# A plain product for the first two groups of a Strassen-tiled step, with its start, its norm steps and its last plans put in another order

## The chip, the cores and the metric

One core of a Trainium2 chip. TensorE (PE; its weight loads are listed as PEld) multiplies, VectorE (DVE) and ScalarE (ACT) do the elementwise work, GpSimd (POOL) and SyncE (SP) mainly issue transfers. Each engine works through its own queue of instructions in order and waits at semaphores for what other engines or transfers have to finish. The metric is device microseconds of one execution. The kernel before took 2694.85 us (median of three runs, 2691.01 to 2695.05).

## The reference

One layer for a prompt of 2048 tokens and, beside it, a sample of 64 tokens with a state; D is 1024, and everything is float32:

```
h = rms_norm(x, g_pre);  vA, bA, cA, zA, q, f, iv, zB, gA, gB = split(h @ w_in)     # ten parts of 1024
u = cA * vA;  yA = (silu(zA) * bA * causal_conv3(u)) @ w_a_out
fg = lb + (1 - lb) * sigmoid(f)
o = hgrn2_scan(state, silu(q) * scale, 1 - fg, iv, log(fg))     # 8 heads, chunks of 64 tokens
yB = (rms_norm_per_head(o) * g_onorm * silu(zB)) @ w_b_out
out = (sigmoid(gA) * yA + sigmoid(gB) * yB) @ w_o
x = x + rms_norm(out, g_post)
y = x + (p @ w_ple_proj) * sigmoid(rms_norm(x, g_ple) @ w_ple_gate)
```

Outputs are y, the last two columns of u and the states after the scan, for prompt and sample.

## The kernel before

**Tiles.** The 2112 tokens are put side by side and cut into three blocks of 704 (`BN`), each block into two halves of 352 (`HN`). Activations lie with features on partitions: tile k holds features 128k to 128k+127 of the 704 tokens. Every float32 operand is split into a hi part (a cast to fp32r, ACT) and a lo part (the difference, DVE; `split`, L184), and a product is three matmuls of 352 columns, hi x hi, hi x lo and lo x hi. Nearly all activations live in one ring of 52 slots (`rt`). PSUM has five banks for the large products (`psg`, named pg) and three (`psa`, named pa) for the scan, the norms and ple.

**Groups.** The ten projections are made by `sgroup` in Strassen-Winograd form: two output columns i1 and i2 of 128 features, times two halves of the tokens, need seven products (`PRODUCTS`) of 4 k-steps x 3 matmuls = 84 matmuls, where the plain form needs 96. The products use sums of weight blocks (S1 to S4) and of activations (T1 to T4). `combined` loads the weights; in block 0 it makes the four weight sums (L295), splits them and keeps sums and lo parts in DRAM (`keep_sum`, `lows`); blocks 1 and 2 load the kept ones (`kept_w`). The activation operands, a list by k for each of B11, T3, T1, T2, B21, T4 and B22, come from `operands`: for each of four pairs (tiles i and i+4) two scaled x tiles (L636), four differences of half tiles (L643 and following) and the splits.

**Stages of a block.** `path_b` goes through the 8 heads: `head_prep` makes three groups (forget gate and query FF/QQ, then the value and output gate), the scan steps of the head hang as `hooks` behind products, and after the first group of a head one step of `fills` is made, which is one group of `gates` (sigmoid of GA and GB, eight groups in all, results spilled to DRAM). `path_a` makes vA, cA, zA, bA and the convolution. Then come w_a_out, w_b_out and w_o (`merge` in block 0, `merge_in_turn` later), `final_norm` (two rms norms with a column sum on TensorE, L581, a power on POOL, and a spread over the partitions by TensorE, L565) and `final_gate`, the last product. `ple` is the small product p @ w_ple_proj: eight steps of 2 halves x 2 k x 3 = 12 matmuls (L951 to L953), each half evicted from its pa bank (L958), the tile spilled to DRAM unless the block is the last.

**Start.** SP's queue loads p of block 0, four ple weights, twelve tiles of x by token (`rows`), four ple weights, then x by feature in pairs with p of block 1 behind the second tile, then weights. Row sums of squares (ACT squares, DVE sums) give the first norm, whose reciprocal root is made on POOL (L555) and spread (L565, `spread_all`). Four steps of block 0's ple are issued between the row sums, the other four behind the spread and the first pair of operands. Then all of p of block 1 is split, and then the pairs 2 to 4 of operands. The first group (GA 0 and 1) runs `by_k`: for each k two steps of block 1's ple and then k of four products.

**Order.** A scheduler places the instructions on the engines by data and priority (`tc.high_priority`); `placed()` holds an instruction behind the last matmul that was issued, `behind_all(marks)` behind the marked instructions. `hook()` pops one entry of `hooks` after each product; `spread_out` fills that list with counts of steps of a generator, here those of `final_norm`, to be run one entry per hook. In blocks 0 and 1 the norm runs amid the gates of the next block; in the last block its first steps (final_norm of half 0) run in the last w_o products (from `(W_O, 4)`) and go on in the last ple, that of half 1 follows amid the last products of `final_gate`. There, too, ACT squares `sum_squares` (L599, L600) and evicts ple (L958), both in its one queue, and DVE adds x (L1088).

Of the kernel before, what the change touches and what calls it, by code (L numbers as in the profile page):

```python
# [82 lines left out]
def hybrid_step(  # L83
# [150 lines left out]
    behind = []  # L234
    last, hooks, copies = [None], [], [None]
# [25 lines left out]
    def steps(gen, n):  # L261
        return lambda: run(gen, n)

# [21 lines left out]
    def combined(i1, i2, first, ahead):  # L285

        with tc.high_priority() if ahead else nullcontext():
# [59 lines left out]
    def sgroup(i1, i2, hc, sink, first, mid=None, by_k=False, ahead=True, between=None):  # L347

        with behind_all(behind.pop(0) if behind else ()):
            w = combined(i1, i2, first, ahead)
# [14 lines left out]
        if by_k:  # L367
            for k in range(KH):
                if between is not None:
                    between()  # L370
                for n in range(4):
                    product(n, (k,))
        for n, (bank, _, _, _, stop) in enumerate(PRODUCTS):
# [9 lines left out]
            if n == 3:  # L383
                u2 = got[0]
                V.tensor_tensor(u2, u2, ps["b"], ALU.add)
            elif n == 4:
                sink(0, 0, ps["a"], None)
            elif n == 5:
                sink(1, 0, u2, ps["c"])
                V.tensor_tensor(got[1], got[1], got[2], ALU.add)  # L390
                sink(1, 1, u2, got[1])
            elif n == 6:
                sink(0, 1, u2, ps["d"])
# [18 lines left out]


# [5 lines left out]
    def operand_of(raw, name, k):  # L419

        (b11, b12), (b21, b22) = ([half(raw[i], h) for h in range(2)] for i in (k, k + KH))
        if name == "B21":
            V.tensor_tensor(b11, b12, b11, ALU.subtract)
        if name == "T2":
# [127 lines left out]
    def rstd_of(ms_ap, out_ap, scale, start=0):  # L552
        V.tensor_scalar(out_ap, ms_ap, scale, EPS, ALU.mult, ALU.add)
        shape = [out_ap.shape[0], out_ap.shape[1]]
        G.tensor_tensor(out_ap, out_ap, mhalf[start : start + shape[0], :].to_broadcast(shape), ALU.pow)  # L555

# [71 lines left out]
    def operands(hc, rs, load, marks=None):  # L628


        for i in range(KH):
            pair = []
            with behind_all(marks[i - 2][1:] if marks and i >= 2 else ()):
                for k in (i, i + KH):
                    xk = load(k)
                    V.scalar_tensor_tensor(xk, xk, g_pre[:, k : k + 1], rs, ALU.mult, ALU.mult)  # L636
                    pair.append(xk)
            (b11, b12), (b21, b22) = ([half(x, h) for h in range(2)] for x in pair)
            one = rt(dt=F32R)
            split(b11, half(one, 0), half(one, 1))  # L640
            hc["B11"].append((half(one, 0), half(one, 1)))
            s = rt()
            V.tensor_tensor(half(s, 1), b22, b12, ALU.subtract)  # L643
            V.tensor_tensor(half(s, 0), b12, b11, ALU.subtract)
            hi, lo = split_rt(s)
            hc["T3"].append((half(hi, 1), half(lo, 1)))
            hc["T1"].append((half(hi, 0), half(lo, 0)))
            t = rt()
            V.tensor_tensor(half(t, 0), b22, half(s, 0), ALU.subtract)
            V.tensor_tensor(half(t, 1), b21, half(t, 0), ALU.subtract)  # L650
            hi, lo = split_rt(t)
            hc["T2"].append((half(hi, 0), half(lo, 0)))
            hc["T4"].append((half(hi, 1), half(lo, 1)))
            hi, lo = rt(dt=F32R), rt(dt=F32R)
            done = split(pair[1], hi, lo)
            if marks is not None:
                marks.append(done)
            hc["B21"].append((half(hi, 0), half(lo, 0)))
            hc["B22"].append((half(hi, 1), half(lo, 1)))
            yield  # L660
# [5 lines left out]
    def gates(bl, hc, kept, first, between=None):  # L666

        for kind in (GA, GB):
            for j in range(0, KB, 2):
                outs = [rt(), rt()]  # L670

                def sink(c, h, x, y):
                    if c == 0:
# [644 lines left out]
```

## Time and profile before

| what | value |
|---|---|
| median of the runs | 2694.85 us |
| the profiled execution: time | 2695.89 us |
| the profiled execution: span | 2694.2 us |
| busy share PE, DVE, ACT, POOL | 98%, 64%, 54%, 13% |
| DMA, mean | 274 GB/s |
| mean granted clock of TensorE | 0.990 |
| PE's busy tenths, first and last of 40 slices | 6 and 9 |

The span goes from the first instruction to the last of the one execution that the profiler recorded; its time is a little more than its span. A row of the timeline or of a group reads: start, duration, engine, line, operation, output<-input, shape; in square brackets the idle time of the engine before it and what ended that. A row of windows reads: the stretch, its length, then busy time and count of each engine (or of PE alone), the granted clock (1 is full speed) and the DMA share and GB/s. Matmuls overlap, so that the duration of one is about twice the distance between two starts; the distances are used here.

### The profile page before, as it was taken

The page shows a single profiled execution, that of the slowest core. Times are in us where ns is not written, and L with a number is a line of the kernel's source. Part 1 is how long each engine was busy: PE and PEld are TensorE (multiplying, and loading weights), DVE is VectorE, ACT ScalarE, POOL GpSimd, SP SyncE. Part 2 cuts the span into 40 slices and gives each one's busy share as a digit, 9 for nine tenths or more (in the row PEclk, how much of TensorE's full clock was granted, in tenths as well). Part 3 has the DMA queues.
Part 4 walks back from the last instruction along what each step waited for, and adds up shares of the span by engine and source line. Part 5 has one row for each costly group of instructions (what it writes and reads, how often), then busy time and mean ns, then how long its engine had stood idle before and what let it go on. Part 6 is the DMA issues. An engine that isn't in the chain of part 4 may idle for free. (4 is left out here: it accounts for less than half of the span.)

```text
span 2694.2 us, 47741 instructions
## 1 busy us (share of the span) xinstructions
PE 2635.0 (98%) x16724; PEld 2607.4 (97%) x16724; DVE 1726.9 (64%) x3340; ACT 1459.7 (54%) x2792; POOL 351.1 (13%) x649
## 2 busy tenths in 40 slices
PE   6999999999999999999999999999999999999989
PEld 5999999999999999999999999999999999999989
DVE  6788888899776543566645577554355564447756
ACT  4665565454334554566645555454466654446654
POOL 1000000110341211011112210021010000001011
PEclk8999999999999999999999999999999999999999
DMA  6767777898997898767789998599876668889855
GB/s 236 267 243 264 267 239 272 281 335 289 338 385 265 314 329 276 243 221 223 223 271 356 388 330 290 182 353 311 269 227 216 222 223 263 274 280 331 281 187 196
DMA packets 362674, 738.16 MB, mean 274 GB/s; under 512 B 44128, under 2 KB 46720, under 8 KB 362432
## 3 DMA queue, kind: packets, MB, share of 16 engines
q1 hardware_dynamic: 325440, 591.34, 65.5%
q0 software_dynamic: 36704, 143.70, 14.7%
q8 instruction: 132, 2.16, 0.3%
q14 instruction: 110, 0.90, 0.1%
q10 hardware_dynamic: 288, 0.05, 0.0%
HBM read 530.43 MB, written 204.49 MB: 273 GB/s over the span
## 5 line engine op out<-in xcount | busy, mean ns | idle before, releaser
L363 PE MATMUL pg<-r,hi 128*128 128x352 f32 x3360 | 1113.6, 332 | 11.9 <-DVE r L411 2.9
L364 PE MATMUL pg<-r,hi 128*128 128x352 f32 x3360 | 1089.8, 324 | 3.9 <-DVE r L184 3.9
L365 PE MATMUL pg<-r,lo 128*128 128x352 f32 x2400 | 778.1, 325 | 3.7 <-DMA lo<-low 3.0
L214 ACT CAST hi<-raw 128x512 fp32r<-128x512 f32 x724 | 447.1, 621 | 579.0 <-PE pg L364 204.3
L363 PEld LDWEIGHTS pg<-r,hi 128*128 128x128 f32 x3360 | 633.8, 189 | 21.5 <-issue 5.1
L364 PEld LDWEIGHTS pg<-r,hi 128*128 128x128 f32 x3360 | 634.5, 189 | 6.7 <-DVE r L184 6.7
L365 PEld LDWEIGHTS pg<-r,lo 128*128 128x128 f32 x2400 | 453.4, 189 | 5.6 <-DMA lo<-low 3.8
L365 PE MATMUL pg<-r,s 128*128 128x352 f32 x960 | 310.4, 323 | 2.7 <-DMA s<-low 2.7
L492 PE MATMUL pg<-r,hi 128*128 128x352 f32 x896 | 290.4, 324 | 0.3 <-DVE r L184 0.3
L491 PE MATMUL pg<-r,hi 128*128 128x352 f32 x896 | 290.2, 324 | 0.4 <-ACT hi L184 0.3
L493 PE MATMUL pg<-r,lo 128*128 128x352 f32 x756 | 245.1, 324 | 2.4 <-DVE lo L184 2.4
L184 ACT CAST hi<-raw 128x512 fp32r<-128x512 f32 (+1 forms) x232 | 141.7, 614 | 173.9 <-PE pg L364 40.7
L184 DVE TENSOR_TENSOR r<-r,r 128x352 fp32r<-128x352 f32 (+3 forms) x270 | 167.5, 640 | 73.1 <-ACT r L184 72.4
L184 DVE TENSOR_TENSOR lo<-raw,hi 128x512 fp32r<-128x512 f32 (+1 forms) x232 | 156.9, 680 | 87.0 <-ACT hi L184 70.7
L184 ACT CAST r<-r 128x352 fp32r<-128x352 f32 (+3 forms) x270 | 148.5, 581 | 72.2 <-DVE r L650 17.0
L365 PEld LDWEIGHTS pg<-r,s 128*128 128x128 f32 x960 | 180.7, 188 | 3.3 <-DMA s<-low 3.3
L459 PE MATMUL pg<-r,hi 128*128 128x352 f32 x560 | 182.1, 327 | 0.1
L458 PE MATMUL pg<-r,hi 128*128 128x352 f32 x560 | 179.9, 326 | 0.0
L184 ACT CAST hi<-s 128x512 fp32r<-128x512 f32 x160 | 99.4, 621 | 147.1 <-PE pg L364 140.4
L491 PEld LDWEIGHTS pg<-r,hi 128*128 128x128 f32 x896 | 168.8, 188 | 1.2 <-ACT r L184 0.7
L492 PEld LDWEIGHTS pg<-r,hi 128*128 128x128 f32 x896 | 168.8, 188 | 0.7 <-DVE r L184 0.6
L379 ACT COPY hf<-pg 128x352 f32<-128x352 f32 x360 | 159.0, 448 | 8.0 <-PE pg L365 7.4
(345 smaller groups left out, 4016.8 us busy)
## 6 DMA issues: line engine op xcount, KB each, us to landing
raw<-w_blk SPq DMA_DIRECT2D x588, 256.0 KB, 4.0
lo<-low SPq DMA_DIRECT2D x413, 256.0 KB, 3.9
raw<-S SPq DMA_DIRECT2D x400, 256.0 KB, 4.0
low<-lo SPq DMA_DIRECT2D x344, 256.0 KB, 3.7
s<-low SPq DMA_DIRECT2D x311, 256.0 KB, 3.9
S<-s SPq DMA_DIRECT2D x160, 256.0 KB, 3.2
r<-w_blk POOLq DMA_DIRECT2D x48, 256.0 KB, 7.5
S<-r POOLq DMA_DIRECT2D x48, 256.0 KB, 6.2
```

Source lines behind the costliest of these rows:

```text
L184: return A.copy(hi, src).ins, V.tensor_tensor(lo, src, hi.bitcast(F32), ALU.subtract).ins
L214: A.copy(hi, raw)
L363: add(hi[:, k, :], xhi, start=start and k == 0, stop=False)
L364: add(hi[:, k, :], xlo, start=False, stop=False)
L365: last[0] = add(lo[:, k, :], xhi, start=False, stop=k == KH - 1).ins
L379: copied = A.copy(got[n], ps[bank])
L458: add(hi[:, k, :], xhi, start=start and k == 0, stop=False)
L459: add(hi[:, k, :], xlo, start=False, stop=False)
L491: T.matmul(ps, hi[:, k % 4, :], xhi[:, c], start=k == ks[0], stop=False)
L492: T.matmul(ps, hi[:, k % 4, :], xlo[:, c], start=False, stop=False)
L493: last[0] = T.matmul(ps, lo[:, k % 4, :], xhi[:, c], start=False, stop=k == ks[-1]).ins
```

## The change

**Plain groups.** A new `plain_group` makes two output columns without sums: 8 k x 2 columns x 2 halves x 3 = 96 matmuls, from the split x tiles themselves, four banks. It is used in block 0 for GB 6 and 7, now the first group of all, and for FF 0 and QQ 0 (head 0's first group). GB 6 and 7 is left out of `gates` of the first block, and no fill is made after head 0's first group there. Since these two groups keep no sums in block 0, `combined` makes and keeps them in block 1 (`first or i1 not in sums`).

**Start.** SP's loads have another order: ple weights 0 to 3, eight row tiles, ple 4 and 5, four row tiles, ple 6 and 7, p of block 1, one x tile, the four weight halves of GB 6 and 7, seven x tiles. All eight steps of block 0's ple are issued ahead of the spread; p of block 1 is split behind the evictions of six of them. The copy of the spread goes half to ACT and half to DVE. `first_operands` works per k: a scaled x (held behind the split of the one two before it), its split in halves, and, from k = 4 on, the sums of that pair (`sums_of`). Two k are made ahead; then each of the eight rounds makes the next k of operands, one step of block 1's ple and one k of the plain group.

**Norm steps.** `spread_out` now puts each entry's steps behind the latest eviction (`copies`, now also ple's) and the latest sum of a group (`adds`). `final_norm` asks for four x tiles ahead instead of two in blocks 0 and 1. In the last block the plans are changed: (0, 0, 1, 0, 1, 1, 1, 1) hang behind the w_o products where it was (0, 1, 0, 1, 1, 1, 2, 2), and (2, 2, 1, 1, 1, 3, 3, 2) in ple where it was (2, 1, 0, 1, 2, 2, 2, 2); each number counts steps run at one hook, so three steps move from w_o into ple.

```diff
-    def combined(i1, i2, first, ahead):
-        with tc.high_priority() if ahead else nullcontext():
+    def combined(i1, i2, first):
+        with tc.high_priority():
...
-        with behind_all(behind.pop(0) if behind else ()):
-            w = combined(i1, i2, first, ahead)
+        w = combined(i1, i2, first or i1 not in sums)
...
-                V.tensor_tensor(u2, u2, ps["b"], ALU.add)
+                adds[0] = V.tensor_tensor(u2, u2, ps["b"], ALU.add).ins
...
+    def plain_group(i1, i2, hs, sink, raws=None, between=None):
+        w, ps = {}, {}
+        def split_of(c, h):
+            key = ((i1, i2)[c], h)
+            raw = raws[c, h] if raws else load_raw(w_blk[key])
+            with nullcontext() if raws else tc.high_priority():
+                w[c, h] = split_w(raw, key)
+        for c, h in ((0, 0), (1, 0)) if between else ((0, 0), (0, 1), (1, 0), (1, 1)):
+            with behind_all(() if between else summed[2 + c]):
+                split_of(c, h)
+        def add(c, ks):
+            for k in ks:
+                hi, lo = w[c, k // KH]
+                for h in range(2):
...
+                    T.matmul(ps[c, h], hi[:, k % KH, :], xhi, start=k == 0, stop=False)
+                    T.matmul(ps[c, h], hi[:, k % KH, :], xlo, start=False, stop=False)
+                    last[0] = T.matmul(ps[c, h], lo[:, k % KH, :], xhi, start=False, stop=k == KB - 1).ins
+        if between:
+            for k in range(KB):
+                between()
+                for c in range(2):
+                    if k == 2:
+                        split_of(c, 1)
+                    with placed():
+                        add(c, (k,))
...
+    def sums_of(hc, pair):
...
+    def first_operands(hc, rs, xs, hs):
+        ends = []
+        for k in range(KB):
+            with behind_all(ends[k - 2][1:] if k >= 2 else ()):
+                scaled_x(xs[k], k, rs)
+            if k < KH:
+                tiles = [rt(dt=F32R) for _ in range(2)]
+                ends.append([split(half(xs[k], h), half(tiles[h], 0), half(tiles[h], 1)) for h in range(2)][-1])
+                hs.append([(half(one, 0), half(one, 1)) for one in tiles])
+            else:
+                hi, lo = rt(dt=F32R), rt(dt=F32R)
+                ends.append(split(xs[k], hi, lo))
+                hs.append([(half(hi, h), half(lo, h)) for h in range(2)])
+                hc["B11"].append(hs[k - KH][0])
+                hc["B21"].append(hs[k][0])
+                hc["B22"].append(hs[k][1])
+                summed.append(sums_of(hc, (xs[k - KH], xs[k])))
+            yield
...
-        sgroup(FF * 8 + hd, QQ * 8 + hd, hc, sink_f, first)
+        if hs and hd == 0:
+            plain_group(FF * 8, QQ * 8, hs, sink_f)
+        else:
+            sgroup(FF * 8 + hd, QQ * 8 + hd, hc, sink_f, first)
...
-        fetch()
-        fetch()
+        for _ in range(2 if bl["last"] else 4):
+            fetch()
...
+        def steps(todo):
+            with behind_all(m for m in copies + adds if m is not None):
+                for gen, n in todo:
+                    run(gen, n)
...
+        ask_ple(0, 1, 2, 3)
+        ask_rows(8)
+        ask_ple(4, 5)
+        ask_rows(4)
+        ask_ple(6, 7)
+        ph1 = load_p(blocks[1], SP)
+        ask_x(1)
+        ask_w(0)
+        ask_w(1)
+        ask_x(7)
...
+    for _ in range(2):
+        with placed():
+            run(first_ple, 1)
+    with behind_all((*done, *copies)):
+        ph, done = split_p(ph1)
+    for _ in range(2):
+        with placed():
+            run(first_ple, 1)
     with behind_all(done):
...
+        rs = rt()
+        cols = [spread(ss[:, 0, 3 * h : 3 * h + 3], HN) for h in range(2)]
+        done = A.copy(half(rs, 0), cols[0]).ins, V.tensor_copy(half(rs, 1), cols[1]).ins
+    run(first_ple)
+    hc, hs = new_operands(), []
+    ops = first_operands(hc, rs, xs, hs)
+    second_ple = ple(blocks[1], ph, kepts[1], held)
+    with behind_all(done):
+        run(ops, 2)
+    def next_k():
+        run(ops, 1)
+        with placed():
+            run(second_ple, 1)
+    outs = [rt(), rt()]
+    with behind_all(done):
+        plain_group(GB * 8 + KB - 2, GB * 8 + KB - 1, hs, gate_sink(outs), w1, next_k)
+    keep_gates(kepts[0], GB, KB - 2, outs)
+    run(second_ple)
+    run(ops)
     constants()
-    fills = gates(blocks[0], hc, kepts[0], True, steps(ple(blocks[1], ph, kepts[1], held), 2))
+    fills = gates(blocks[0], hc, kepts[0], True)
...
-                    spread_out((norms[0], (0, 1, 0, 1, 1, 1, 2, 2)))
+                    spread_out((norms[0], (0, 0, 1, 0, 1, 1, 1, 1)))
...
-            spread_out((norms[0], (2, 1, 0, 1, 2, 2, 2, 2)), (norms[1], (0,) * 6 + (1, 1) + (2, 2, 2, 2, 1, 0, 1, 3, 3, 2)))
+            spread_out((norms[0], (2, 2, 1, 1, 1, 3, 3, 2)), (norms[1], (0,) * 6 + (1, 1) + (2, 2, 2, 2, 1, 0, 1, 3, 3, 2)))
```

## The prediction, made before the changed kernel had run

> **What bounds the kernel now.** I read the page's busy shares, then the waits of PE, then busy time and granted clock by stretches, then the timelines of the first 110 us and of the last 110 us.
>
> ```profile
> PE 2635.0 (98%) x16724; PEld 2607.4 (97%) x16724; DVE 1726.9 (64%) x3340; ACT 1459.7 (54%) x2792; POOL 351.1 (13%) x649
> PE pa L951 <- ACT r L958: 10.5, 2, 5.9
> PE pa L565 <- POOL rows L555: 4.5, 1, 4.5
> ```
>
> TensorE bounds nearly the whole span, so only its idle stretches and its slow clock can be won. Where these lie:
>
> ```profile
> 0.00:105.08 105.08, 78.97 (x372) 0.85 0.69 243
> 44.27:47.68 3.41, 2.47 (x11) 1.00 0.90 305
> 47.68:51.10 3.42, 1.61 (x5) 1.00 0.99 323
> 51.10:54.50 3.40, 2.38 (x6) 0.50 0.32 122
> 54.50:57.90 3.40, 2.81 (x7) 0.50 0.00 0
> 68.10:71.60 3.50, 3.50 (x14) 0.50 0.51 179
> 920.00:930.00 10.00, 7.08 (x43) 6.50 (x41) 6.66 (x10) 4.10 (x8) 3.17 (x6) 1.00 1.04 410
> 930.00:935.20 5.20, 4.86 (x20) 4.86 (x21) 1.26 (x3) 1.21 (x3) 0.00 (x0) 0.67 1.03 401
> 2598.70:2604.90 6.20, 0.29 (x2) 0.00 (x1) 6.20 (x15) 2.71 (x7) 0.00 (x0) 0.95 0.22 66
> 2604.90:2614.50 9.60, 8.24 (x28) 7.79 (x29) 3.69 (x10) 3.57 (x9) 0.88 (x1) 0.50 0.11 28
> ```
>
> (Rows with one pair of busy figures show PE, clock, DMA; the others PE, PEld, DVE, ACT, POOL, clock, DMA.) Two cadences of a 352-column matmul:
>
> ```profile
> 9.01 0.49 PE L953 MATMUL pa<-r,r 128*128 128x352 f32 x1
> 9.30 0.49 PE L951 MATMUL pa<-r,r 128*128 128x352 f32 x1
> 13.80 0.32 PE L952 MATMUL pa<-r,r 128*128 128x352 f32 x1
> 17.66 0.32 PE L952 MATMUL pa<-r,r 128*128 128x352 f32 x1
> 22.60 2.93 PE L565 MATMUL pa<-ident,rows 128*128 128x128 f32 x12 [4.46 <-POOL rows L555]
> ```
>
> At full clock 24 of them take 17.66-13.80 = 3.86 us, 0.161 each; at clock 0.50 one takes 0.29. The first 105.08 us hold 372 matmuls: 12 of the spread (L565) and 360 of 352 columns, which at 0.161 are 58 us. So some 45 us of TensorE are lost before 105, more than everywhere else together. The clock fell at 51.1 after a stretch with 1.61 of 3.42 us busy, did not fall after 2.47 of 3.41, did not rise after 2.81 of 3.40, and rose after 3.50 of 3.50.
>
> **The change, part by part.** Durations are from the one profiled execution (span 2694.2, time 2695.89 us, 1.04 above the runs' median of 2694.85); the sum is made against its time.
>
> *Start.* The two plain groups have 8 blocks x 2 columns x 2 halves x 3 = 96 matmuls each, for 7 x 4 x 3 = 84: 24 more, 3.9 us, in the counts below. So I compare when the 360th (before) and the 384th (after) is begun; what is left then is the same.
>
> (a) Before, 48 matmuls of block 0's ple stand ahead of the spread; after, all 96. The first 48 stay as they were (begun up to 17.82). The next 48 take 7.7 us, to 25.5, instead of the 4.46 wait, the spread, and 4.6 of waiting at L951 later. They need the held splits and three PSUM banks; evictions (0.38 each on ACT, row below) keep that up within 0.5 us. Row sums pass the held splits on DVE, so POOL's power is done by 22, hidden. The spread took 2.93 at clock 0.50; 1.6 at full: to 27.1. Its two copies go to ACT and DVE at once, where ACT had both.
>
> (b) Eight rounds: a step of block 1's ple (12 matmuls) and one k of the plain group (12), 3.86 us on PE. The pace is DVE and ACT:
>
> ```profile
> 47.01 0.95 DVE L636 SCALAR_TENSOR_TENSOR r<-r,vec,r 128x704 f32<-128x704 f32 x1
> 47.87 0.69 DVE L184 TENSOR_TENSOR lo<-s,hi 128x512 fp32r<-128x512 f32 x1
> 48.47 0.69 DVE L295 TENSOR_TENSOR s<-raw,s 128x512 f32<-128x512 f32 x1
> 49.08 0.52 DVE L184 TENSOR_TENSOR r<-r,r 128x352 fp32r<-128x352 f32 x1
> 49.51 0.52 DVE L643 TENSOR_TENSOR r<-r,r 128x352 f32<-128x352 f32 x1
> 56.97 0.52 DVE L643 TENSOR_TENSOR r<-r,r 128x352 f32<-128x352 f32 x1
> 65.60 0.52 DVE L643 TENSOR_TENSOR r<-r,r 128x352 f32<-128x352 f32 x1
> 31.94 1.46 ACT L184 CAST r<-r 128x704 fp32r<-128x704 f32 x2 [1.95 <-DVE r L650]
> 33.31 1.15 ACT L958 COPY r<-pa 128x352 f32<-128x352 f32 x3
> 32.75 1.69 DVE L184 TENSOR_TENSOR r<-r,r 128x704 fp32r<-128x704 f32 x2 [0.84 <-ACT r L184]
> ```
>
> From start to start DVE takes 0.86 for a scaled x, 0.60 for a weight split or sum, 0.43 for a half tile, and 0.85 (1.69/2) for a whole-tile split; ACT 0.73 and 0.38. The first k waits: spread 27.1, copy 27.65, a weight split, two scaled x to 30.0, splits and the second weight's lo to 32.4; PE, done with ple step 0 at 29.0, does 12 matmuls between 29.0 and 32.9 (2 us lost). Up to the lo split of x7 DVE's queue then holds 6 scaled x (5.2), 4 half splits (1.7), 10 whole-tile splits (8.5), 4 weight splits (2.4) and 12 half differences (5.2): 23 us, with some 1 us of waiting for ACT 56. x7 and its k would come in time for PE alone (58). But ACT's queue has evictions of ple behind the pairs' sums: step 3's wait for the split of T of pair 2 (DVE at 47.2, ACT 48.0), step 4's for that of pair 3 and two weights (53.7), step 5's for pair 4 (58.4, ACT 59.1). With three banks, PE waits for each: 45.4 to 48.4 (3.0), 52.3 to 54.15 (1.85), 58.0 to 59.45 (1.45). From there 42 matmuls are left of the rounds: 59.45 + 6.8 = 66.2. The clock may fall at such waits (3.0 idle in 3.41 is under the 1.61 of 3.42 that made it fall); the slower matmuls then partly fill the next wait. Ends: 0, and 3.0 for two such stretches (half of 3.41 each); I take 1.4.
>
> (c) The second plain group needs no further operand; its weights are split by 64 to 68: 96 x 0.161 = 15.4, to 81.6, with the clock's 1.4 83.0. Its cover is that the combined group behind it has sums and splits ready by 70; DVE had 32% idle and more after 75 and loses 8 weight sums. Against 105.08: -22.1.
>
> Queues: SP issues 36 loads ahead of the next weights as before, but p of block 1, x0 and four weights before x1 to x7: about 9.5 MB up to x7, landed by 28 at the 244 to 400 GB/s that the first 30 us moved; x7 is scaled at 46. POOL's spills of ple move with ple, 8 issues in 40 us.
>
> *Sums in block 1.* FF 0 and GB 6 left no kept sums, so block 1 makes them: 4 sums and 4 more lo splits a group, 4.8 us of DVE, and SP's stores among its loads. Cover:
>
> ```profile
> 1090.00:1100.00 10.00, 10.00 (x72) 9.98 (x71) 1.79 (x4) 5.47 (x10) 1.08 (x2) 1.00 0.93 287
> ```
>
> DVE is 18% busy there. Ends 0 and 9.6 (no cover at all); I take +0.5, since products wait up to 12 us behind their group's start.
>
> *Norm steps of blocks 0 and 1.* They go behind the latest eviction and sum, and four x tiles are fetched ahead, not two. In 920 to 935 PE lost 2.9 of 10 us and then half of 3.41 to the clock; DMA was full (1.04), DVE waited for x twice:
>
> ```profile
> 915.38 0.89 DVE L1088 TENSOR_TENSOR r<-r,r 128x704 f32<-128x704 f32 x1 [2.32 <-DMA r<-x_fm]
> 923.95 0.89 DVE L1088 TENSOR_TENSOR r<-r,r 128x704 f32<-128x704 f32 x1 [2.26 <-DMA r<-x_fm]
> ```
>
> Those two DVE waits go, but PE itself waited for weights (lo<-low), and two early x tiles of 352 KB on POOL's queue share the same full DMA. Ends -5 (all that is lost there) and +5 (as much again); I take -1.5.
>
> *End.* Three of norm 0's eight first steps move from the last out products into ple of the last block.
>
> ```profile
> 2598.67 0.32 PE L953 MATMUL pa<-r,lo 128*128 128x352 f32 x1
> 2604.90 0.66 PE L951 MATMUL pa<-r,hi 128*128 128x352 f32 x1 [5.91 <-ACT r L958]
> 2608.39 1.44 PE L581 MATMUL pa<-ones,r 128*128 128x1 f32 x6 [1.36 <-DVE r L600]
> 2603.57 0.93 ACT L599 ACTIVATE r<-r 128x352 f32<-128x352 f32 x2 [1.41 <-DVE r L1088]
> 2604.42 0.79 ACT L958 COPY r<-pa 128x352 f32<-128x352 f32 x2
> ```
>
> The first eviction (L958) stands behind six squares, each behind a DVE step; loss 6.1 + 1.7, and 28 matmuls at 0.29 in 2604.9 to 2614.5, 3.7 to 4.4: 12 us. After, it stands behind three: j=2's sum of DVE comes at 2600.0, the eviction at 2600.5, PE waits 2.2; later evictions stand behind two squares (1.5 more, 0.6 at the sum of squares): 4.3. With a slow stretch of 2 us, the gain is 5.7; the chain to the gate (1.58 us a block) then has PE's matmuls beside it as now. Ends -12 and +3; I take -5.5.
>
> Sum: 2695.9 - 22.1 + 0.5 - 1.5 - 5.5 = 2667.3; less part of the 1.04, 2667.
>
> The row 47.68:51.10 made the clock fall though TensorE never stood still for all of it. The Trainium skill, "TensorE: Matmul & The Clock Gate", section "Part 1: The HAM clock gate", has the clock fall after an idle window of about 3.4 us; by that none of the waits of 3.0 or less costs clock, and the sum would be 1.4 less. That is a rival below, and the row speaks against it.
>
> **Rivals.** (1) The clock holds through the rounds: 81.6 for 83.0, 2665.6. For it: 2.47 of 3.41 did not make it fall. (2) The end gains nothing, the wait is only split over later evictions: 2672.5. For it: DVE was busy for all 6.20 us of that wait, and the same DVE steps remain. (3) Half clock through all rounds, as from 51.1 to 71.6: 24 x 0.294 = 7.06 a round, 27.1 + 56.5 + 15.4 = 99.0, a gain of 6.1: 2683. Against it: PE would then have no waits, and a full stretch raised the clock. (4) Slower: the rounds are a closed loop, pair splits, eviction, bank, matmul, each round as long as a pair was before (56.97 to 65.60, 8.6) and the three ACT splits of 0.73 that its evictions stand behind, 10.8: 27.1 + 86.4 + 15.4 = 128.9, 2713. It decides from 9.3 us a round. Against it: a round holds only half a pair.
>
> **Numbers.** Forecast 0.53, (1) 0.12, (2) 0.18, (3) 0.11, (4) 0.06. Range 2658 to 2682: the ends of block 1, of the norms and of the end on both sides, and (2); most of (3) and (4) is out. 0.2% is 5.4 us, about what a measurement here can tell: faster 0.92, within 0.02, slower 0.06.
>
> **What would show it.** Right: the spread at 25 to 26; 396 matmuls begun by 83; PE's waits for ple evictions there 5 to 8 us; the last ple's longest wait under 3 and the slow stretch of 9.6 shorter; no PE wait for a split lo in block 1. Wrong: a clock of 0.50 from 30 to 66, rounds over 6 us, or new DMA waits near 920 and 1790.

## The result, and the profile after

The changed kernel takes 2666.72 us (median of six runs, 2662.58 to 2670.51); the kernel before took 2693.98 beside it (2689.19 to 2695.05). The ratio is 0.9902, with a 95% interval of 0.989 to 0.9913, so 23 to 30 us are gained. The profiled execution of the changed kernel is the one of 2662.58 us, 4 below its median, so part of what the two profiles differ by is chance, and the parts below are compared over several kernels.

The page of the changed kernel, its busy line and where PE stands:

```profile
span 2660.9 us, 47751 instructions
PE 2621.2 (99%) x16748; PEld 2601.6 (98%) x16748; DVE 1725.0 (65%) x3337; ACT 1453.1 (55%) x2786; POOL 350.4 (13%) x649
```

24 matmuls more than before (16724), as counted ahead. To see where time went, I count matmuls of 352 columns and take the time at which the same point of the work is reached: the end of the start (before: 360 begun; after: 384), the 400 matmuls behind it, 1200 matmuls around the norm of block 0 and of block 1, and the last 800. Durations in us, worked out from the starts of PE's rows:

| stretch | before | after | difference | predicted |
|---|---|---|---|---|
| start | 105.08 | 83.56 | -21.5 | -22.1 |
| the next 400 | 78.75 | 79.99 | +1.2 | 0 |
| sums of FF 0 and GB 6 in block 1 | | | 0 | +0.5 |
| norm of block 0 | 205.13 | 201.58 | -3.6 | -1.5 for both |
| norm of block 1 | 203.89 | 201.22 | -2.7 | |
| the last 800, with the end | 152.34 | 148.16 | -4.2 | -5.5 |
| all the rest | 1949.0 | 1946.4 | -2.6 | 0 |

The rest is nearly the same code in both; over the profiles of all fourteen kernels of this document it took between 1942 and 1951 us, so its -2.6 is no effect. It also holds the sums of FF 0 and GB 6 in block 1.

The windows of the start of the changed kernel (length, PE busy, PEclk, DMA share, GB/s), the first being all of it, the others the stretches of 3.41 us around its waits. (The record of the clock begins at 11.13 us here; time ahead of it counts as full, though matmuls start 0.29 apart there, at 9.22, 9.52 and 9.81, as they do at half clock.)

```profile
0.00:83.56 83.56, 70.25 (x396) 0.96 0.77 279
28.20:31.61 3.41, 1.53 (x7) 1.00 1.02 408
45.27:48.69 3.42, 2.13 (x14) 1.00 0.00 2
52.10:55.51 3.41, 1.45 (x10) 1.00 0.01 5
55.51:58.92 3.41, 3.41 (x12) 0.50 0.72 223
```

And PE's waits there, from the timeline (start, duration, instruction, in brackets the idle time before it and what ended it):

```profile
29.44 0.82 PE L427 MATMUL pg<-r,hi 128*128 128x352 f32 x2 [0.72 <-ACT r L184]
31.40 0.50 PE L428 MATMUL pg<-r,hi 128*128 128x352 f32 x1 [1.15 <-DVE r L184]
49.29 0.43 PE L1018 MATMUL pa<-r,r 128*128 128x352 f32 x1 [1.89 <-ACT r L1025]
55.38 0.56 PE L1018 MATMUL pa<-r,r 128*128 128x352 f32 x1 [1.96 <-ACT r L1025]
61.23 0.43 PE L1018 MATMUL pa<-r,r 128*128 128x352 f32 x1 [0.19 <-ACT r L1025]
```

The 4.5 us wait for the first norm is gone, the wait for the first k is 1.9, and three waits for evictions of ple (L1025, L958 before) stand at the three steps where the prediction put them, about 1 to 2 us later than it had them, at 4.0 in sum for its 6.3. The clock was at half twice, from 31.61 and from 55.51, where before it was for 6.8, 3.4 and 20.5 us.

The end of the changed kernel, PE's waits in the last ple and behind it:

```profile
2573.52 0.43 PE L1018 MATMUL pa<-r,hi 128*128 128x352 f32 x1 [3.79 <-ACT r L1025]
2580.58 0.61 PE L614 MATMUL pa<-ones,r 128*128 128x1 f32 x4 [0.44 <-DVE r L633]
2615.33 0.94 PE L598 MATMUL pa<-ident,cols 128*128 128x128 f32 x6 [0.94 <-POOL cols L587]
```

The wait of 5.91 before is 3.79, and that for the sum of squares (L581 before, L614 now) went from 1.36 to 0.44.

### The profile page after: what moved, and what is told of

Its sections match the earlier page's. It is cut to its first block, busy times and chain, and to the rows that moved or that the text cites. A ratio compares the mean times of both kernels' runs of the same rounds, so it can differ in the third digit from the quotient of the medians.

```text
span 2660.9 us, 47751 instructions
## 1 busy us (share of the span) xinstructions
PE 2621.2 (99%) x16748; PEld 2601.6 (98%) x16748; DVE 1725.0 (65%) x3337; ACT 1453.1 (55%) x2786; POOL 350.4 (13%) x649
## 4 chain that ended last, share of the span: by engine, by line
PE 89%; DMA 4%; DVE 3%; issue 2%; ACT 1%; POOL 1%; SPq 0%; DVEq 0%; ACTq 0%; POOLq 0%
PE pg L357 19%; PE pg L359 19%; PE pg L358 19%; PE pg L525 4%; PE pg L524 4%; PE pg L523 4%; PE pg L490 3%; PE pg L491 3%; PE pg L492 3%; PE pa L921 1%; PE pa L957 1%; DMA r<-w_blk 1%; PE pa L911 1%; PE pa L959 1%; DMA s<-low 1%
## 5 line engine op out<-in xcount | busy, mean ns | idle before, releaser
L357 PE MATMUL pg<-r,hi 128*128 128x352 f32 x3304 | 1093.1, 331 | 6.8 <-DVE r L403 2.7
L358 PE MATMUL pg<-r,hi 128*128 128x352 f32 x3304 | 1067.4, 323 | 0.0
L359 PE MATMUL pg<-r,lo 128*128 128x352 f32 x2356 | 761.9, 323 | 0.0
L357 PEld LDWEIGHTS pg<-r,hi 128*128 128x128 f32 x3304 | 621.8, 188 | 12.7 <-DVE r L865 4.6
L358 PEld LDWEIGHTS pg<-r,hi 128*128 128x128 f32 x3304 | 622.3, 188 | 0.0
L359 PEld LDWEIGHTS pg<-r,lo 128*128 128x128 f32 x2356 | 442.8, 188 | 0.0
L524 PE MATMUL pg<-r,hi 128*128 128x352 f32 x896 | 290.2, 324 | 0.2 <-DVE r L184 0.2
L523 PE MATMUL pg<-r,hi 128*128 128x352 f32 x896 | 289.8, 324 | 0.0
L525 PE MATMUL pg<-r,lo 128*128 128x352 f32 x756 | 245.4, 325 | 2.8 <-DVE lo L184 2.8
L491 PE MATMUL pg<-r,hi 128*128 128x352 f32 x560 | 181.7, 326 | 0.0
L490 PE MATMUL pg<-r,hi 128*128 128x352 f32 x560 | 179.4, 325 | 0.0
L524 PEld LDWEIGHTS pg<-r,hi 128*128 128x128 f32 x896 | 169.0, 189 | 0.7 <-DVE r L184 0.5
L523 PEld LDWEIGHTS pg<-r,hi 128*128 128x128 f32 x896 | 168.7, 189 | 0.6 <-ACT r L184 0.5
```

The lines of the kernel that those rows point to most:

```text
L357: add(hi[:, k, :], xhi, start=start and k == 0, stop=False)
L358: add(hi[:, k, :], xlo, start=False, stop=False)
L359: last[0] = add(lo[:, k, :], xhi, start=False, stop=k == KH - 1).ins
L490: add(hi[:, k, :], xhi, start=start and k == 0, stop=False)
L491: add(hi[:, k, :], xlo, start=False, stop=False)
L523: T.matmul(ps, hi[:, k % 4, :], xhi[:, c], start=k == ks[0], stop=False)
```

## The experiments

**The start alone.** The changed kernel with all norm steps as before.

```diff
-            with behind_all(m for m in copies + adds if m is not None):
-                for gen, n in todo:
-                    run(gen, n)
+            for gen, n in todo:
+                run(gen, n)
...
-        for _ in range(2 if bl["last"] else 4):
+        for _ in range(2):
...
-spread_out((norms[0], (0, 0, 1, 0, 1, 1, 1, 1)))
+spread_out((norms[0], (0, 1, 0, 1, 1, 1, 2, 2)))
...
-spread_out((norms[0], (2, 2, 1, 1, 1, 3, 3, 2)), ...
+spread_out((norms[0], (2, 1, 0, 1, 2, 2, 2, 2)), ...
```

> The changed kernel with its norm steps as before: no marks in spread_out, two x tiles ahead, both plans of the last block as before. What is left of the change is the start, the plain groups and the sums in block 1. Theory (the terms of the sum add up, and the start has nearly all): the 384th matmul of 352 columns begins at 83 to 84 as in the changed kernel, PE's waits near 905, 1760 and 2570 are those of the kernel before, and the time is 2673 to 2677, 6 to 10 above the changed kernel. Rival (norms and end gain nothing, the rest of the difference of the two profiles is chance): 2666 to 2668.

Measured: 2675.73 us (2673.97 to 2676.62), 0.9934 of before [0.992, 0.9948]. The theory holds: by the two ratios 18 of the 26 us are the start, 9 are the norm steps and the end. The waits of the last ple are those of the kernel before (5.90 and 1.26 us, for 5.91 and 1.36).

**The order of the norm steps.** The first two edits of the diff above; the plans of the last block stay as changed.

```diff
-            with behind_all(m for m in copies + adds if m is not None):
-                for gen, n in todo:
-                    run(gen, n)
+            for gen, n in todo:
+                run(gen, n)
...
-        for _ in range(2 if bl["last"] else 4):
+        for _ in range(2):
```

> The changed kernel without the marks in spread_out and with two x tiles ahead in every block; the plans of the last block stay as changed. Theory (the order and the earlier x tiles shorten the DMA waits of the products behind them): PE loses again 3 to 4 us to waits for s and lo near 905 and 2.5 near 1760, the time is 2669 to 2672. Rival (these waits are chance of the transfers and of the clock): the time is 2666 to 2668.

Measured: 2672.04 us (2668.0 to 2676.41), 0.9919 [0.9906, 0.9933], 5 above the changed kernel's median and at the upper end of the theory's range. The intervals of the two ratios just meet, but the stretches decide. The 1200 matmuls around block 0's norm took 203.5 to 205.7 us in the four kernels with the old order (before, the start alone, this one, and "block 0's ple early" below) and 200.4 to 202.2 in the ten with the new; around block 1's 203.7 to 206.1 and 200.6 to 203.9. The medians differ by 3.7 and 2.9: 6.6 us in sum; the time of this run is 5.3 longer. PE's waits in all of that stretch of block 0, before, after and with the start alone (waits view: line, what it waited for, us in total, times, longest):

```profile
PE pg L365 <- DMA lo<-low: 2.1, 1, 2.1
PE pg L365 <- DMA s<-low: 1.2, 1, 1.2
PE pg L363 <- ACT hi L214: 0.7, 1, 0.7
```
```profile
PE pg L359 <- DMA s<-low: 1.4, 1, 1.4
PE pg L357 <- ACT hi L214: 0.7, 1, 0.7
```
```profile
PE pg L359 <- DMA lo<-low: 1.5, 2, 1.0
PE pg L359 <- DMA s<-low: 0.8, 1, 0.8
PE pg L357 <- ACT hi L214: 0.7, 1, 0.7
PE pg L357 <- ACT hf L371: 0.3, 1, 0.3
PE pa L614 <- DVE r L633: 0.2, 1, 0.2
```

With the new order the wait for a lo part is gone and one of 1.4 stays. In this run PE waits 3.5 us there, 2.1 of them for lo parts. Over all profiles the four with the old order have 3.3 to 4.0 us of waits around block 0's norm, and each of them waits for a lo part; the ten with the new order have 0.7 to 2.1, and none of them does. By the medians that is about 2 of the 3.7 us; what the rest is was not found. Whether the marks or the two x tiles more do it was not tried apart.

**The plans of the last block.** The changed kernel with both plans as before, and nothing else.

```diff
-spread_out((norms[0], (0, 0, 1, 0, 1, 1, 1, 1)))
+spread_out((norms[0], (0, 1, 0, 1, 1, 1, 2, 2)))
...
-spread_out((norms[0], (2, 2, 1, 1, 1, 3, 3, 2)), ...
+spread_out((norms[0], (2, 1, 0, 1, 2, 2, 2, 2)), ...
```

> The changed kernel with both plans of the last block as before (eight steps in the last out products, twelve in ple). Theory (three squares fewer ahead of the first eviction are worth 4 us): PE waits 6 us for the first eviction of the last ple, the clock is at half for 6.8 to 10 us, the time is 2670 to 2672. Rival (the end gains nothing, the wait is only split over later evictions): 2666 to 2668, and with the marks the old plan has a wait as short as the new.

Measured: 2670.93 us (2664.01 to 2674.08), 0.9913 [0.9899, 0.9927], and the last 800 matmuls take 151.85 us against 148.16. The theory: 3.7 us are the plans. The intervals of the ratios overlap here too, and again the stretches decide: the last 800 took 151.9 to 152.8 us in the four kernels with the old plans and 148.0 to 148.9 in the seven that have the changed ones and nothing else new at the end. With the marks in place the old plan waits as long as in the kernel before:

```profile
2580.44 0.66 PE L1018 MATMUL pa<-r,hi 128*128 128x352 f32 x1 [5.90 <-ACT r L1025]
2583.82 1.44 PE L614 MATMUL pa<-ones,r 128*128 128x1 f32 x6 [1.25 <-DVE r L633]
```

**Two more steps moved into ple.** If three steps are worth 3.7 us, are five worth more?

```diff
-spread_out((norms[0], (0, 0, 1, 0, 1, 1, 1, 1)))
+spread_out((norms[0], (0, 0, 1, 0, 1, 0, 1, 0)))
...
-spread_out((norms[0], (2, 2, 1, 1, 1, 3, 3, 2)), ...
+spread_out((norms[0], (3, 2, 1, 2, 1, 3, 3, 2)), ...
```

> The changed kernel with two more norm steps moved from the last out products into ple: (0,0,1,0,1,0,1,0) and (3,2,1,2,1,3,3,2). Theory (the squares ahead of the first eviction are the cause of its wait, and VectorE's work is the same): the wait of 3.8 near 2569 falls to under 2.2, the clock does not fall at 2574, the gain is 2 to 4, time 2663 to 2665. Rival (VectorE is the bound of that stretch, so that the wait comes back at later evictions or at the sum of squares): 2666 to 2668; slower if the norm ends later than ple: up to 2670.

Measured: 2668.92 us (2668.12 to 2672.03), 0.9911 [0.9897, 0.9925]; the last 800 matmuls take 153.08, 4.9 more than in the changed kernel. That profile is of the slowest execution (2672.03); the medians differ by 2.2, and the intervals overlap. The rival holds, a little above its time: the first wait is 2.09, as the theory had it, but two others have taken its place.

```profile
2578.73 0.43 PE L1018 MATMUL pa<-r,hi 128*128 128x352 f32 x1 [2.09 <-ACT r L1025]
2582.54 0.66 PE L1018 MATMUL pa<-r,hi 128*128 128x352 f32 x1 [0.87 <-ACT r L1025]
2586.96 1.22 PE L614 MATMUL pa<-ones,r 128*128 128x1 f32 x5 [2.29 <-DVE r L633]
```

The clock was at half for 13.65 us (2579.89 to 2593.54) instead of 3.41. In this profile the wait was split, and the split waits cost more clock than the one.

**Squares' sums on GpSimd.** If VectorE bounds the last ple, taking work off it should show that.

```diff
-            V.tensor_tensor(acc, acc, sq, ALU.add)
+            adder.tensor_tensor(acc, acc, sq, ALU.add)      # adder = G for the second norm of the last block, else V
```

> The changed kernel with the additions of squares of the second norm of the last block (line 633) on GpSimd instead of VectorE. Theory (VectorE bounds the stretch from the last out products through ple, and each eviction of ple waits behind squares that wait for VectorE): eight additions of 0.43 a norm leave VectorE, the wait of 3.8 near 2569 falls to 2.0 to 2.9, the waits behind it do not grow, time 0 to 4 below the changed kernel's 2667. Rival (GpSimd's additions are slower and end later): the wait for the first eviction shrinks, but TensorE waits for the sum of squares behind ple, 2667 to 2672.

Measured: 2675.31 us (2674.3 to 2677.26), 0.9926 [0.9911, 0.9941]. Worse than the rival's range, and the first wait did not shrink either (4.08). An addition of 128x352 takes GpSimd twice VectorE's 0.52 us, and it stands in one queue with the issues of x:

```profile
2572.93 1.16 POOL L633 TENSOR_TENSOR r<-r,r 128x352 f32<-128x352 f32 x1 [10.92 <-ACT r L632]
2574.03 0.57 POOL L1146 DMA_DIRECT2D r<-x_fm  x1
2575.59 1.04 POOL L633 TENSOR_TENSOR r<-r,r 128x352 f32<-128x352 f32 x1 [0.98 <-ACT r L632]
```

PE then waits 1.88 us for the first sum of squares and 5.07 for that of the second half. By these rows the chain of scaled tile, square and sum is what is long there; the experiment doesn't tell whether VectorE's share alone bounds it.

**The first groups in Strassen form again.** First both, with all else of the start kept.

```diff
-        plain_group(GB * 8 + KB - 2, GB * 8 + KB - 1, hs, gate_sink(outs), w1, next_k)
+        sgroup(GB * 8 + KB - 2, GB * 8 + KB - 1, hc, gate_sink(outs), True, by_k=True, raws=w1, between=next_k)
...
-            run(second_ple, 1)
+            run(second_ple, 2)
```

> The changed kernel with both plain groups in Strassen form again: GB 6 and 7 by k with the sums of its weights and pairs of operands made as before, two ple steps of block 1 a pair, x tiles loaded in pairs; FF 0 and QQ 0 too. All else of the start (96 ple matmuls ahead of the spread, p of block 1 split behind them, the load order) stays. Theory (the plain form is worth its 24 matmuls, since a first k of four products needs four weight sums and a whole pair ready): 24 matmuls fewer, 3.9 us, but VectorE has 4.8 us of weight sums and 5.6 of a pair ahead of the first k, and 7 to 8 us a pair behind it against 5.8 on TensorE; the point where 360 matmuls are begun comes 2 to 8 us later than the 384th of the changed kernel, the time is 2669 to 2675. Rival (the gain of the start is that of ple moved ahead and amid, the form of the group is worth nothing): 2663 to 2667.

Measured: 2681.3 us (2678.11 to 2683.64), 0.9958 [0.9941, 0.9975]; 360 matmuls are begun by 95.48 us, 12 later than the 384 of the changed kernel. That is later than the theory's 2 to 8, and the time is above its range. Two rows show what TensorE and VectorE waited for:

```profile
53.03 0.66 PE L1022 MATMUL pa<-r,r 128*128 128x352 f32 x1 [23.67 <-ACT r L1029]
38.92 0.69 DVE L294 TENSOR_TENSOR s<-raw,s 128x512 f32<-128x512 f32 x1 [3.88 <-DMA S<-s]
```

ple's first evictions stood behind the splits of two pairs, and these behind the weight sums, of which one waited 3.88 us until the store of an earlier sum had landed (second row); that is a part of the 23.67. So it is not the form alone that was measured, but the form with its place in ScalarE's queue; another order might do better.

Then only the second:

```diff
-        if hs and hd == 0:
-            plain_group(FF * 8, QQ * 8, hs, sink_f)
-        else:
-            sgroup(FF * 8 + hd, QQ * 8 + hd, hc, sink_f, first)
+        sgroup(FF * 8 + hd, QQ * 8 + hd, hc, sink_f, first)
```

> The changed kernel with only the second plain group, FF 0 and QQ 0, in Strassen form again: 12 matmuls fewer, its four sums and their splits made in block 0 as before. Theory (the plain form there buys time for the operands' sums, whose last split ends at 63.8, and for the weights' sums): the 1.9 us of 12 matmuls come back, but VectorE's 4.8 us of sums stand ahead of it at 58 to 66; the two about cancel, time 2665 to 2669. Rival 1 (all of it is hidden): 2664 to 2665. Rival 2 (the sums are late, TensorE waits as for the first groups of the kernel before): 2670 to 2674.

Measured: 2674.63 us (2674.24 to 2676.11), 0.9934 [0.9919, 0.9949]: rival 2, a little above its time. With 12 matmuls fewer the kernel is 8 us slower. PE waits 3.59 and 3.83 for the first k: its loads and sums have got among those of the first rounds, where a scaled x now waits 3.82 for its tile and a weight sum 3.94 for its weights. Another 3.95 are lost up to 111.9 us, for a sum of the group's results that stands behind weight sums and splits on VectorE. So here, too, the form was measured with its place in the queues.

**Block 0's ple early, alone.** One part of the start, put into the kernel before.

```diff
             for j in (n + 2,) if n < 3 else (5, 6, 7):
                 done = held_split(j)
+    with placed():
+        run(first_ple)
...
         run(ops, 1)
-    run(first_ple)
```

> The kernel before with one part of the change: the last four steps of block 0's ple (48 matmuls) ahead of the spread instead of behind it and the first pair. Theory (the gain of the start is that of the rounds and of the plain form, which need only single x tiles): the spread comes 3 us later and with it all operands, VectorE bounds what follows, so the 360th matmul of 352 columns begins between 102 and 108 against 105.1, time 2691 to 2697. Rival (moving ple into the wait for the first norm is most of the start's gain): 360th matmul at 85 to 95, time 2675 to 2685.

Measured: 2688.2 us (2683.25 to 2689.9), 0.9967 [0.9956, 0.9979]; 360 matmuls are begun by 101.23, 3.9 earlier than before. The time is a little below the theory's range, the start just short of it (102 to 108), and the rival (85 to 95) falls; the other 5 us of this kernel's gain lie elsewhere and were not followed. At the start PE is busy ahead of the spread and then stands still for 8.66 us for the first pair.

```profile
36.68 1.25 PE L951 MATMUL pa<-r,r 128*128 128x352 f32 x3 [8.66 <-ACT r L184]
```

**ple ahead of the operands in each round.**

```diff
     def next_k():
-        run(ops, 1)
         with placed():
             run(second_ple, 1)
+        run(ops, 1)
```

> The changed kernel with one swap in the rounds: the step of block 1's ple is issued ahead of that round's scaled x, splits and pair sums, so that ScalarE's evictions stand ahead of them in its queue. Theory (the order in ScalarE's queue is the cause of TensorE's waits of 2 us for evictions): the waits near 47, 53 and 61 go, the clock does not fall at 55.5, the 384th matmul begins 3 to 6 us earlier than 83.4, time 2661 to 2664. Rival (VectorE, busy 9 to 10 of each 10 us from 28 to 58, sets the pace): TensorE waits as long for the splits of the later k instead, 2666 to 2669.

Measured: 2660.63 us (2657.04 to 2667.49), 0.9884 [0.9868, 0.99], which is not clear of the changed kernel's interval. The median lies just below the theory's range and well below the rival's. The profiled execution, however, is the slowest of the four, 2667.49; the others took 2657.04 to 2661.77. In it the waits at 47 and 53 are gone (one of 0.18 is left), one of 1.90 stands at 57.94 and one of 0.29 at 63.91, the 385th matmul begins at 82.44 for 83.56, and at the end of the next 400 nothing is left of it (163.83 for 163.55). So the order of the evictions was the cause of the two waits. In this profile it is not what bounds the start, as the rival says, though TensorE waited for an eviction again and not for the splits of the later k. The other three times speak for the theory, and no profile shows one of them: whether this order gains anything is open.

**Idle matmuls in the waits.** Does the slow clock cost what I put it at? Twelve matmuls on a spare bank, in two waits:

```diff
+                if j in (4, 5) and s is bl["segs"][1]:      # block 1's ple only
+                    spare = ps_gemm()
+                    for i in range(12):
+                        last[0] = T.matmul(spare, hi[:, 0, :], ph[0][0][:, c], start=i == 0, stop=i == 11).ins
```

> The changed kernel with 12 matmuls on a spare bank, whose result nobody reads, ahead of the second half of steps 4 and 5 of block 1's ple, where TensorE waits 2 us for a bank. Theory (the clock goes by the busy share of each stretch of 3.41 us, a fall costs 1.7 us): with 1.9 of each wait filled the stretch from 52 to 55.5 is busy for over 3 of 3.41, the clock does not fall near 55.5, the waits themselves stay at nothing, the 384th real matmul begins 1.7 us earlier, time 2664.5 to 2666. Rival (the fillers delay what stands behind them, or the fall comes at the next wait): 2667 to 2670.

Measured: 2661.51 us (2659.53 to 2668.37), 0.9889 [0.9874, 0.9904]. The clock did as the theory had it, the start did not gain:

```profile
52.00:55.40 3.40, 3.39 (x22) 1.00 0.00 0
55.40:58.80 3.40, 3.40 (x21) 1.00 0.69 214
58.80:62.20 3.40, 1.62 (x10) 1.00 0.76 277
```

The clock stayed at 1.00, and 384 real matmuls were begun by 83.67, as by 83.56 in the changed kernel. The 1.7 us of the slow stretch turn up as a wait of 1.78 at 61.33, which was 0.19: PE had got ahead of the split that this eviction stands behind. The median is below the theory's range (2664.5 to 2666), but the start did not bring it.

With idle matmuls in all waits (12 ahead of the first k, 12 in ple's steps 4, 5 and 6, 24 in step 1 of the last ple):

```diff
+                if j in fill and s is bl["segs"][1]:
+                    filler(hi, ph[0][0][:, c], fill[j])      # as above, fill[j] matmuls
...
+            if len(hs) == 3:
+                filler(held[0][0], ph[0][0][:, :HN], 12)     # next_k, behind the first step of ple
...
-    second_ple = ple(blocks[1], ph, kepts[1], held)
+    second_ple = ple(blocks[1], ph, kepts[1], held, fill={4: 12, 5: 12, 6: 12})
...
-            run(ple(bl, ph, kept))
+            run(ple(bl, ph, kept, fill={1: 24}))
```

> The changed kernel with idle matmuls, whose result nobody reads, in all the waits of the start and of the last ple: 12 ahead of the first k of the plain group, 12 ahead of the second half of steps 4, 5 and 6 of block 1's ple, 24 in step 1 of the last ple. Theory (a stretch of 3.41 us in which TensorE is busy for less than about half costs 1.7 us of clock behind it): the clock does not fall near 32, 55 and 2574, where the changed kernel lost 1.7 each; 5 us below the changed kernel in the profile's stretches, time 2660 to 2663. Rival (the fillers shift the waits rather than fill them): 2664 to 2669.

Measured: 2667.23 us (2665.45 to 2667.59), 0.9894 [0.9879, 0.9908]: the rival's range. The clock never fell in the start, which ended at 83.77; the last 800 real matmuls took 150.61 us, 2.5 more than in the changed kernel, with waits of 1.17 and 1.34 behind the fillers, and the clock fell there all the same.

**The pairs' sums behind all rounds.**

```diff
-                summed.append(sums_of(hc, (xs[k - KH], xs[k])))
             yield
+        for k in range(KH):
+            summed.append(sums_of(hc, (xs[k], xs[k + KH])))
+            yield
```

> The changed kernel with the pairs' sums (four half differences and two whole-tile splits a pair) behind all eight k of scaled x and splits instead of amid them; the first two pairs come in rounds 6 and 7, the others behind the first plain group. VectorE's work is the same, the plain groups do not need these sums. Theory (TensorE's waits of 2 us in the rounds come from pair sums ahead of evictions and of the next k): the two or three waits of 2 us between 45 and 62 go, the 384th matmul begins at 79 to 81 against 83.4, and as VectorE is done at 62 as now the gain stays, time 2662 to 2664. Rival (VectorE's total work to the third group is the bound): the 384th begins as early, but TensorE waits for sums at the third group or at the first scan, so that at the 760th nothing is left, 2666 to 2669.

Measured: 2667.41 us (2663.84 to 2668.3), 0.9893 [0.9875, 0.9911]: no change. Seven of the eight rounds ran with no wait, and then came the whole of it:

```profile
38.00:48.00 10.00, 10.00 (x64) 10.00 (x63) 6.56 (x9) 3.81 (x8) 1.62 (x3) 1.00 0.75 273
48.00:58.00 10.00, 10.00 (x64) 10.00 (x63) 6.25 (x11) 5.29 (x11) 1.41 (x3) 1.00 0.20 79
58.00:68.00 10.00, 6.22 (x36) 5.65 (x35) 6.74 (x11) 6.83 (x13) 2.65 (x6) 0.96 0.37 144
```
```profile
66.00 0.43 PE L427 MATMUL pg<-r,hi 128*128 128x352 f32 x1 [3.30 <-ACT hi L184]
67.23 0.63 PE L429 MATMUL pg<-r,lo 128*128 128x352 f32 x1 [0.47 <-DVE lo L184]
```

(Columns of the windows: PE, PEld, DVE, ACT, POOL, clock, DMA.) Neither theory had the place: VectorE is busy for only 62 to 67% here. PE waits for the weights of the second plain group, whose splits are held behind the third pair's sums (`behind_all(summed[2 + c])`), and those now come late. That the 4 us would be won with that hold moved too is argued from this row, not tried.

## Why the prediction was right

The time, 2667 for 2666.72, is closer than its steps: the norms gave 5 us more than the forecast, and the start, the matmuls behind it and the end gave less. That these cancel to within 0.3 us is luck; that most of the gain lies at the start is not.

Of the signs named for being right, the spread (25.3), the slow stretch at the end (3.41 us) and block 1 without a wait for a split lo came, and 396 matmuls were begun by 83.56 for 83. Two did not: PE's waits for evictions of ple at the start were 4.0 us, not 5 to 8, and the longest wait of the last ple was 3.79, not under 3.

*Start.* (a) Block 0's ple ended at 25.3 and the spread at 26.8, for 25.5 and 27.1, and what (a) is worth alone is 3.9 us.

(b) The mechanism held: three waits for evictions behind pairs' splits, at the steps named, at 1.9, 2.0 and 0.2 for 3.0, 1.85 and 1.45. The third ended at 61.2 for 59.45. The clock's 1.4 was put behind it and was not spent there: two stretches fell ahead of it, each worth 1.7 us of matmuls, and with idle matmuls the start ended no earlier when the second did not fall (83.67) and when neither did (83.77). That slower matmuls fill the next wait, as the prediction says, shows in the profiles: in the changed kernel the clock fell behind the second of the three waits and the third was 0.2; with two more steps moved and with sums on GpSimd it fell behind the first, and the second was 0.4; in the other three kernels with this start it fell behind the third, and all three waits were 1.8 to 2.0.

(c) 83.56 for 83.0, in part because the late third eviction and the unspent 1.4 cancel. Over the six kernels with this start unchanged it was 83.56 to 86.09, so -19 to -21.5 is a fairer figure than -22.1; the spread of 2.5 us lies in the first k's wait and in these three waits. The 400 matmuls behind it took 1.2 more than before; "what is left then is the same" was not quite so, since a wait of 0.7 of the scan's first transposes (L901) for a sum of VectorE (L403) stands at 101 us now.

*Sums in block 1.* Of +0.5, nothing was seen. They run at 1011 to 1062 us, not at 1090 to 1100 where the prediction took VectorE's cover from, and VectorE was busy for 30.57 of 55 us there. PE was busy for all of it:

```profile
L291 DVE TENSOR_TENSOR s<-raw,raw x4: 685/692/693, 1011.1 to 1055.4; 128x512 f32<-128x512 f32 x4
1010.00:1065.00 55.00, 55.00 (x344) 55.00 (x343) 30.57 (x51) 28.62 (x50) 4.31 (x8) 1.00 0.81 269
```

*Norm steps.* This term was mis-sized: -1.5 with ends at -5 and +5, and -6.6 us by the medians of fourteen profiles, which is outside its ends. I took the PE waits in 920 to 935 as the most that could be had in one block and discounted them, since DMA was full there. Full it was afterwards too (0.99 over 875 to 945), and the wait for lo was gone; block 1's norm, 2.9, I hadn't counted beside it.

*End.* -4.2 for -5.5. The step that failed is "an eviction behind three squares at 2600.5, PE waits 2.2": it stood behind three squares of norm 0, but VectorE's sums, scalings and splits ahead of each made it 3.79. ScalarE's rows for the second and the third square and the eviction (L632 and L1025) show it waiting for VectorE's addition of x (L1155):

```profile
2570.33 0.89 ACT L632 ACTIVATE r<-r 128x352 f32<-128x352 f32 x2 [1.07 <-DVE r L1155]
2572.63 0.50 ACT L632 ACTIVATE r<-r 128x352 f32<-128x352 f32 x1 [1.41 <-DVE r L1155]
2573.03 0.79 ACT L1025 COPY r<-pa 128x352 f32<-128x352 f32 x2
```

That the gain is the three moved steps, as said, is shown by the plans put back (+3.7). Rival 2 in its first half (the end gains nothing) falls; in its second half (the wait is only split over later evictions) it is what the next two steps did.

The rivals on the clock: that it holds through the rounds was not so, yet holding it with idle matmuls changed nothing; half clock through all rounds and rounds of 9.3 us were not seen, a round took 3.9 us (12 and 12 matmuls) without its wait.

## What to carry to other kernels

Moving work within the same chain may split a wait and not shorten it: three norm steps moved into the last ple gained 3.7 us, five gained no more. Look at what the engine behind the wait does through all of it, and expect the wait at the next hand-over, as there and with the pairs' sums. A slow clock ahead of a wait for another engine can cost nothing, as at this start (83.67 and 83.77 for 83.56), so its price is known only from where the next operand is ready. A plain product that needs one operand at a time can beat a cheaper form with sums at the very start, where in one group 12 more matmuls were worth 8 us as its loads and sums were placed here.

## What the runs showed of the hardware

In these traces the clock of TensorE is granted by stretches of 3.41 us, and by how busy TensorE was in the stretch. Within a profile all changes lie a whole number of stretches apart (31.61, 35.03, 55.51 and 58.92 in the changed kernel); against the kernel's start they lie elsewhere in another profile (33.55, 36.96 and 50.61 with two more steps moved). Over all fourteen profiles every stretch at full clock with less than 1.5 us busy was followed by one at half clock; between 1.5 and 2.1 both were seen; above 2.1 it held, but for four stretches of 2.69 to 2.81 at the norms of blocks 0 and 1, each with twelve tiny matmuls of 128x1 (1.47 us) among the busy time. A stretch at half clock with 2.82 us busy or less was followed by another; from 2.90 on the clock rose, with two exceptions (3.17 and 3.41). The rows above show the fall from both sides: 1.53 and 1.45 fell, 2.13 held. The kernel before has its examples in the prediction, 1.61 and 2.47. The Trainium skill, "TensorE: Matmul & The Clock Gate", section "Part 1: The HAM clock gate", names a free-running window of 3413 ns, and the stretches agree with its length; that it takes an idle window to fall does not agree, as a wait of 1.96 us was enough. So the same wait may make the clock fall in one execution and not in the next: with 1.45 us busy in the stretch of the second ple wait the clock fell in the changed kernel, and with 1.52, 1.56 and 1.59 it held in three kernels with the same start. A stretch at half clock is 1.7 us of matmuls (half of 3.41). Whether this makes a part of the 8 us between the fastest and the slowest run of one kernel was not measured.
